# Gate matrices from 64 packed columns: one matmul per token in place of two

## The chip, the cores and the metric

The kernel runs on one core of one Trainium2 chip. The metric is the device time of one execution in microseconds, lower is better. A core has five engines with a queue of their own each: PE (TensorE, matmuls; its weight loads are listed as PEld), DVE (VectorE), ACT (ScalarE), POOL (GpSimd) and SP (SyncE, which issues most of the DMAs here). PE reads SBUF and writes PSUM, which has eight banks of 128 x 512 float32 words.

## The reference

Two layers of a decoder trunk over 1040 positions (16 meta tokens and 1024 real ones) of width 1024. Each layer adds a token mixer (sliding-window attention, stick-breaking attention and gated linear attention side by side) and then a PEER feed-forward block with 4096 experts. Only the second block matters here:

```python
s = einsum('thpd,hpnd->thpn', (xt @ wq).reshape(t, 8, 2, 128), sub_keys)
s_top, i_top = top_k(s, 16)                      # per head, on 64 keys twice
best_s, best_j = top_k(all sums of two of them, 16)
idx = expert numbers of the best 16, for 8 heads   # 128 per token
g = softmax(best_s)
a = gelu((xt @ u.T)[idx]) * g
w = zeros(t, 4096).at[token, idx].add(a)
out = w @ v
```

So each token has 128 chosen experts with a gate each. The kernel computes gelu(xt @ u.T) for all 4096 experts, and multiplies it by a dense gate matrix that is zero but at the chosen experts.

## The kernel before, in words

Matrices are held transposed, with features on the 128 partitions and positions along the free dimension. Float32 products go through three matmuls of rounded high and low parts. The positions of a layer are taken as two halves, each of two quarters: the first half is the object `P` (528 positions in layer 0, 512 in layer 1), the second half `Q` (512). `peer_setup` sets `first` to True for P and to False for Q.

`hidden` (L1117 is its matmul) computes the 4096 expert activations as 32 rows of 128 experts. A row is 24 matmuls of 128 x 512 into one PSUM bank, and then a gelu on ACT into `G`, an array of [128, 32 rows, positions]. For positions whose gates are there already, the gelu goes to a buffer (L1123) and POOL multiplies it by the gates that stand in `G` (L1124); for the others it goes into `G` (L1126). The weights are copied to a rounded form on ACT (L310) as they come in.

`gates` makes the dense gates of 16 positions in one call. An expert number is split in two: m, one of 128 (the partition), and r, one of 32 (the row). The 128 slots of a position (8 heads by 16 choices) lie on the partitions, and for each position a matmul sums over the slots: (slots x 128, a one-hot matrix `Lh` of m) transposed, times (slots x 32, the one-hot matrix `R0` of r times the gate). The gate is held as two float16 numbers, a high and a low part, scaled by 2^15 (`GSC`), so `R` has two parts. DVE builds Lh (L1156, 128 x 2048 float16), R0 (L1159, 128 x 512) and R (L1161, 128 x 1024). PE then does 32 matmuls of 32 columns (L1168), for each position the high and the low part into the same 32 columns of a bank, so that PSUM adds them. One bank holds the 16 positions. DVE multiplies the rows that `hidden` has finished by the gates, straight from PSUM, with the scale taken out (L1173); ACT copies the gates of the later rows into `G` (L1175). Lh, R0 and R have two buffers each; the PSUM ring "g" has banks 0 and 1.

`hidden(l, Q, G, HQ, 32, "hq", cst, QE)` (L1358) calls `gates` after its rows, so many that the 32 calls of the second half are spread evenly over rows 8 to 30; the rows use the ring "hq", banks 4 to 7. Before it `combine` makes m, r and the gates on DVE (its lines L1063 and L1098 write float16 elements that don't lie side by side), and `slots` brings them to the slots' layout. After it `values` multiplies `G` by v, for which all gates must be there.

Each buffer has a fixed place in one of two arenas by a table of names. `s` holds the scores of the product keys, 3072 words; in the last layer the rows `hs` are loaded into its place (L1387) after the second half's scores are done with. The order of the instructions on each engine is not that of the program: a planner orders them by a timeline that it works out itself before the launch. An engine then runs its queue strictly in that order, and an instruction that waits holds up those behind it. Buffers that overlap are kept in the order of the program by waits.

Of the kernel before, what the change touches and what calls it, by code (L numbers as in the profile page):

```python
# [12 lines left out]
F32 = mybir.dt.float32  # L13
F32R = mybir.dt.float32r
F16 = mybir.dt.float16
BF16 = mybir.dt.bfloat16
U32 = mybir.dt.uint32
AF = mybir.ActivationFunctionType
ALU = mybir.AluOpType
# [16 lines left out]
GSC = float(2 ** 15)  # L36
# [23 lines left out]
def tile_trunk(ctx, tc, h0, w_pk, wgate, w2, glab, w_out, wqT, keysT, u_pk, v_w, sinks,  # L60
               n_attn, n_ffn, n_mix, n_fin, out):
    nc = tc.nc
    ACT, DVE, POOL, PE, SP = nc.scalar, nc.vector, nc.gpsimd, nc.tensor, nc.sync
# [9 lines left out]
    place = {}  # L73
    NG = 12

    def lay(ar, plan, o, lim=None):
        for t, e, b in plan:
            e = (e + 7) // 8 * 8
            at = place.setdefault(t, [ar, [], 0])[1]
            while len(at) < b and (lim is None or o + e <= lim):  # L80
                at.append(o)
                o += e
        return o
# [8 lines left out]
    for t in ("ah", "al"):  # L92
# [8 lines left out]
    o = lay(1, [("G", G_EL, 1), ("s", 3072, 1)], g0)  # L101

    o = max(lay(1, [("L", 1024, 2), ("R0", 256, 2), ("R", 512, 2)], o),
            lay(1, [(t, e, 1) for t, e in [("X", 1536), ("C", 768), ("W", 192), ("J", 192), ("qi", 192), ("rmx", 12),
                                           ("rsr", 12)] + [(f"rt{i}", 96) for i in range(8)]], o))
# [13 lines left out]
    kb, bb = place["keep"][1], place["beta"][1]  # L119

    place["h5"] = [1, [place["ht"][1][0] + i * 272 for i in range(5)], 0]
    place["xa"] = [1, [place["fac"][1][0] + i * 272 for i in range(4)], 0]
    place["xb"] = [1, [place["L"][1][0] + i * 272 for i in range(7)], 0]
    place["hs"] = [1, [place["s"][1][0]], 0]
# [14 lines left out]
    def sb(shape, dt, tag, bufs=1):  # L139
        pl = place[tag]  # L140
        off = pl[1][pl[2] % len(pl[1])]
        pl[2] += 1
        n = 1
        for x in shape[1:]:
            n *= x
        words = (n * (2 if dt in (F16, BF16) else 4) + 3) // 4
        assert (dt == F32R) == (pl[0] == 0), tag
        a = arenas[pl[0]][0:shape[0], off:off + words]
        if dt not in (F32, F32R):
            a = a.bitcast(dt)  # L150
        a = a[:, 0:n]
        if len(shape) == 3:
            a = a.rearrange("p (a b) -> p a b", b=shape[2])
        elif len(shape) == 4:
            a = a.rearrange("p (a b c) -> p a b c", b=shape[2], c=shape[3])
        elif len(shape) == 5:
            a = a.rearrange("p (a b c d) -> p a b c d", b=shape[2], c=shape[3], d=shape[4])
        return a
# [4 lines left out]
    def set_rings(**kw):  # L163
        for tag, bs in kw.items():
            rings[tag] = [bs, 0]

    def ps1(tag="a"):
        r = rings[tag]
        r[1] += 1
        return banks[r[0][(r[1] - 1) % len(r[0])]]  # L170

    set_rings(d=(0, 1), o=(2,), a=(3, 4, 5, 6, 7), h=(6, 7, 2, 3), hq=(4, 5, 6, 7), g=(0, 1), s=(4, 5), v=(4, 5, 6, 7, 2, 3))


    ident = const.tile([128, 128], F32, name="ident")
# [762 lines left out]
    def peer_setup(qa, qb, first):  # L938

        P = Layer()  # L940
        P.sp = Span(qa.c0, qb.c1)
        P.parts = [(0, qa), (qa.w, qb)]
        P.merge = qa.w == qb.w
        P.sall = sb([128, 3072], F32, "s")
        P.s0 = sb([128, 1536], F32, "s0")
        P.first = first
        P.mT, P.rT = [[sb([128, 272], F16, t) for i in range(2)] for t in ("mT", "rT")]
        P.gg = [sb([128, 68, 2, 4], F16, "gg") for i in range(2)]
        P.mS = sb([128, 3, 128], F16, "mS")
        P.rS = sb([128, 3, 128], F16, "rS")  # L950
        P.gS = sb([128, 3, 128], F32, "gS")
        P.V = {}
        P.rows = 0
        P.gated = [0, 0]
        return P
# [150 lines left out]
    def hidden(l, P, G, lo, hi, ring, cst=None, end=32):  # L1106

        cs = cuts(P, (0, 1))
        for r in range(lo, hi):
            pss = [ps1(ring)[:, 0:w] for h, o, w in cs]  # L1110
            for k in range(KT):
                if k % 4 == 0:
                    wh, wl = wpiece(u_pk[l, r][:, k * 128:(k + 4) * 128], f"u{l}_{r}_{k // 4}")
                ks = slice(k % 4 * 128, k % 4 * 128 + 128)
                for i, (wt, low) in enumerate(((wh, 0), (wh, 1), (wl, 0))):
                    for ps, (h, o, w) in zip(pss, cs):
                        PE.matmul(ps, wt[:, ks], yv(h, low, k, 0, w // 2 if h is None else w),  # L1117
                                  start=(k == 0 and i == 0), stop=(k == KT - 1 and i == 2))
            for ps, (h, o, w) in zip(pss, cs):
                n = min(max(sum(P.gated) - o, 0), w)  # L1120
                if n:
                    ga = sb([128, w], F32, "h5" if w <= 272 else "ht")
                    ACT.activation(ga[:, 0:n], ps[:, 0:n], AF.Gelu)  # L1123
                    POOL.tensor_tensor(G[:, r, o:o + n], ga[:, 0:n], G[:, r, o:o + n], op=ALU.mult)  # L1124
                if n < w:
                    ACT.activation(G[:, r, o + n:o + w], ps[:, n:w], AF.Gelu)  # L1126
            P.rows = r + 1
            while cst and sum(P.gated) < P.sp.w and sum(P.gated) * (end - lo) < P.sp.w * (r + 1 - lo):
                gates(P, int(P.gated[0] == P.parts[0][1].w), G, *cst)
# [16 lines left out]
    def gates(P, half, G, iotaM, iotaR):  # L1146


        t0 = P.gated[half]
        go = P.parts[half][0] + t0  # L1150

        def v4(a, n):
            return a[:, t0:t0 + 16].rearrange("p (b t) -> p b t", t=4).unsqueeze(2).to_broadcast([128, 4, n, 4])

        Lh = sb([128, 4, 128, 4], F16, "L", 2)
        DVE.tensor_tensor(Lh, iotaM.unsqueeze(1).to_broadcast([128, 4, 128, 4]), v4(P.mT[half], 128), op=ALU.is_equal)  # L1156

        R0 = sb([128, 4, 32, 4], F16, "R0")
        DVE.tensor_tensor(R0, iotaR.unsqueeze(1).to_broadcast([128, 4, 32, 4]), v4(P.rT[half], 32), op=ALU.is_equal)  # L1159
        R = sb([128, 4, 2, 32, 4], F16, "R")  # L1160
        DVE.tensor_tensor(R, R0.unsqueeze(2).to_broadcast([128, 4, 2, 32, 4]),  # L1161
                          P.gg[half][:, t0 // 4:t0 // 4 + 4].unsqueeze(3).to_broadcast([128, 4, 2, 32, 4]), op=ALU.mult)
        n = P.rows
        ps = ps1("g")
        for i in range(16):
            b, t = i // 4, i % 4
            for part in range(2):
                PE.matmul(ps[:, i * 32:(i + 1) * 32], Lh[:, b, :, t], R[:, b, part, :, t], start=(part == 0),  # L1168
                          stop=(part == 1))
        pv = ps.rearrange("p (t r) -> p r t", r=32)  # L1170
        if n:
            gv = G[:, 0:n, go:go + 16]
            DVE.scalar_tensor_tensor(gv, pv[:, 0:n], 1.0 / GSC, gv, op0=ALU.mult, op1=ALU.mult)  # L1173
        if n < 32:
            ACT.activation(G[:, n:32, go:go + 16], pv[:, n:32], AF.Copy, scale=1.0 / GSC)  # L1175
        P.gated[half] = t0 + 16
# [71 lines left out]
    hq = sb([128, KT, 272], F32, "hq")  # L1248
# [22 lines left out]
    for l in range(DEPTH):  # L1271
# [3 lines left out]
        P = peer_setup(qs[0], qs[1], True)  # L1275
# [39 lines left out]
        G = sb([128, 32, 528], F32, "G")  # L1315
# [68 lines left out]
        o, sp = Q.parts[1]  # L1384
# [63 lines left out]
```

## Time and profile before

| | |
|---|---|
| median of 3 runs | 3275.61 us (3270.31 to 3278.28) |
| profiled execution | 3277.03 us, its span 3275.3 us, mean granted clock 0.967 |
| PE busy | 3116.9 us (95%) |
| DVE busy | 2062.4 us (63%) |
| ACT busy | 1368.4 us (42%) |
| POOL busy | 980.8 us (30%) |
| gate matmuls (L1168) | 4128, of which 1024 in the second half of each layer |

Busy times come from one profiled execution. The span runs from the first to the last instruction. An instruction's own time can reach over the start of the next one on the same engine, so busy times of a stretch are less than the sum of the durations. "Idle before" is the time in which the engine did nothing ahead of an instruction, with what ended it.

### The profile page before, as it was taken

The page shows a single profiled execution, that of the slowest core. Times are in us where ns is not written, and L with a number is a line of the kernel's source. Part 1 is how long each engine was busy: PE and PEld are TensorE (multiplying, and loading weights), DVE is VectorE, ACT ScalarE, POOL GpSimd, SP SyncE. Part 2 cuts the span into 40 slices and gives each one's busy share as a digit, 9 for nine tenths or more (in the row PEclk, how much of TensorE's full clock was granted, in tenths as well). Part 3 has the DMA queues.
Part 4 walks back from the last instruction along what each step waited for, and adds up shares of the span by engine and source line. Part 5 has one row for each costly group of instructions (what it writes and reads, how often), then busy time and mean ns, then how long its engine had stood idle before and what let it go on. Part 6 is the DMA issues. An engine that isn't in the chain of part 4 may idle for free.

```text
span 3275.3 us, 65889 instructions
## 1 busy us (share of the span) xinstructions
PE 3116.9 (95%) x23453; PEld 2625.9 (80%) x23453; DVE 2062.4 (63%) x6694; ACT 1368.4 (42%) x3120; POOL 980.8 (30%) x976
## 2 busy tenths in 40 slices
PE   8999999989899999999998999999889999899998
PEld 7686887769899998888885878786768888688788
DVE  4645445689886299763325554558796736986457
ACT  4554434423334344324445544334333344443354
POOL 5314021323455242020501141213144524302136
PEclk9898999989999999999998999999799999999999
DMA  8676775637445665546766887667454467554655
GB/s 269 224 254 213 233 272 177 218 114 252 132 137 185 184 194 185 162 140 204 266 202 194 291 268 243 230 208 229 165 176 142 156 196 229 185 175 142 213 180 168
DMA packets 406443, 655.57 MB, mean 200 GB/s; under 512 B 44560, under 2 KB 122464, under 8 KB 406112
## 3 DMA queue, kind: packets, MB, share of 16 engines
q1 hardware_dynamic: 406112, 651.35, 61.7%
q8 instruction: 184, 3.01, 0.4%
q14 instruction: 147, 1.20, 0.1%
HBM read 492.70 MB, written 158.47 MB: 199 GB/s over the span
## 4 chain that ended last, share of the span: by engine, by line
PE 37%; DVE 9%; DMA 2%; ACT 1%; issue 1%; POOL 0%; SPq 0%; POOLq 0%; DVEq 0%; ACTq 0%
PE b L1207 10%; PE b L1117 9%; PE b L339 7%; PE b L1168 2%; PE b L991 2%; PE b L707 1%; PE b L761 1%; DVE arena_r L1201 1%; DVE arena L1001 1%; PE b L622 1%; DVE arena L1004 1%; DVE arena L1002 1%; DMA arena<-in_v_w_dram 1%; PE b L743 0%; PE b L584 0%
## 5 line engine op out<-in xcount | busy, mean ns | idle before, releaser
L283 POOL TENSOR_TENSOR arena_r<-arena,arena_r 128x512 fp32r<-128x512 f32 (+1 forms) x440 | 568.7, 1297 | 844.7 <-ACT arena_r L276 763.8
L1207 PE MATMUL b<-arena_r 128*128 128x512 f32 (+2 forms) x4224 | 742.1, 335 | 23.7 <-DVE arena_r L1201 17.9
L1117 PE MATMUL b<-arena_r 128*128 128x512 f32 (+2 forms) x3840 | 759.3, 356 | 5.1 <-DVE arena L263 5.1
L1207 PEld LDWEIGHTS b<-arena_r 128*128 128x128 f32 x4224 | 640.0, 189 | 114.1 <-DVE arena_r L1201 25.3
L339 PE MATMUL b<-arena_r 128*128 128x256 f32 (+1 forms) x4992 | 694.9, 294 | 22.7 <-DVE arena L361 6.8
L1117 PEld LDWEIGHTS b<-arena_r 128*128 128x128 f32 x3840 | 623.4, 190 | 102.1 <-DVE arena L263 5.7
L339 PEld LDWEIGHTS b<-arena_r 128*128 128x128 f32 x4992 | 638.2, 194 | 58.9 <-issue 22.9
L276 ACT ACTIVATE arena_r<-arena 128x512 fp32r<-128x512 f32 x456 | 286.1, 629 | 492.5 <-POOL arena_r L283 116.4
L1201 DVE TENSOR_TENSOR arena_r<-arena,arena_r 128x512 fp32r<-128x512 f32 (+2 forms) x352 | 274.1, 794 | 328.8 <-ACT arena_r L1200 328.3
L310 ACT ACTIVATE arena_r<-arena 128x512 fp32r<-128x512 f32 x392 | 246.1, 630 | 432.5 <-issue 132.5
L991 PE MATMUL b<-arena_r 128*128 128x256 f32 (+1 forms) x1632 | 209.1, 283 | 2.7 <-DMA arena_r<-m_0l 1.3
L991 PEld LDWEIGHTS b<-arena_r 128*128 128x128 f32 (+1 forms) x1632 | 197.0, 183 | 12.3 <-issue 4.3
L1124 POOL TENSOR_TENSOR arena<-arena 128x32 f32<-128x32 f32 (+25 forms) x91 | 106.1, 1174 | 286.5 <-ACT arena L1175 261.7
L1156 DVE TENSOR_TENSOR arena<-arena 128x2048 f16<-128x2048 f16 x129 | 171.4, 1331 | 21.4 <-PE b L1168 21.4
L259 POOL TENSOR_TENSOR arena<-arena 128x256 f32<-128x256 f32 (+1 forms) x126 | 110.2, 875 | 248.9 <-ACT arena L258 248.8
L1200 ACT ACTIVATE arena_r<-arena 128x512 fp32r<-128x512 f32 (+2 forms) x352 | 172.1, 502 | 29.8 <-PE b L1207 26.2
L1173 DVE SCALAR_TENSOR_TENSOR arena<-b,arena 128x224 f32<-128x224 f32 (+20 forms) x129 | 63.7, 500 | 151.1 <-PE b L1168 146.8
L1168 PEld LDWEIGHTS <-arena 128*128 128x128 f16 x4128 | 144.2, 118 | 16.9 <-issue 13.7
L719 DVE TENSOR_TENSOR_SCAN arena<-arena,zf 128x272 f32<-128x272 f32 (+6 forms) x116 | 105.1, 908 | 75.1 <-ACT arena L714 74.3
L1168 PE MATMUL b<-arena 128*128 128x32 f16 x4128 | 152.1, 190 | 0.0
L283 DVE TENSOR_TENSOR arena_r<-arena,arena_r 128x256 fp32r<-128x256 f32 (+1 forms) x140 | 75.3, 541 | 98.5 <-ACT arena_r L276 87.3
L580 POOL TENSOR_TENSOR arena<-arena,mhalf 128x8 f32<-128x8 f32 (+3 forms) x43 | 62.7, 1459 | 231.3 <-DVE arena L577 150.9
(269 smaller groups left out, 3826.3 us busy)
## 6 DMA issues: line engine op xcount, KB each, us to landing
arena<-in_v_w_dram SPq DMA_DIRECT2D x288, 256.0 KB, 2.9
arena<-in_u_pk_dram SPq DMA_DIRECT2D x256, 256.0 KB, 3.0
arena<-in_w_pk_dram SPq DMA_DIRECT2D x144, 256.0 KB, 4.6
arena_r<-a_0l SPq DMA_DIRECT2D x108, 256.0 KB, 4.0
arena_r<-a_1l SPq DMA_DIRECT2D x108, 256.0 KB, 3.8
arena<-m SPq DMA_DIRECT2D x96, 256.0 KB, 4.4
arena<-h SPq DMA_DIRECT2D x192, 128.0 KB, 3.2
arena_r<-a_0h SPq DMA_DIRECT2D x72, 256.0 KB, 3.5
```

Source lines behind the costliest of these rows:

```text
L259: POOL.tensor_tensor(acc, acc, sq[:, 0:sp.w], op=ALU.add)
L276: ACT.activation(hi, src, AF.Copy)
L283: e.tensor_tensor(lo[:, a:b], src[:, a:b], hi[:, a:b].bitcast(F32), op=ALU.subtract)
L310: ACT.activation(hi, wload(src), AF.Copy)
L339: PE.matmul(ps, wt[:, ks], x.at(low, k, xo, sp.w), start=(k == 0 and i == 0), stop=(k == KT - 1 and i == 2))
L991: PE.matmul(ps, yv(half, low, k, o, m), wt[:, kk * 256:kk * 256 + 256], start=(k == 0 and i == 0 and e == 0), stop=(k == KT - 1 and i == 2 ...
L1117: PE.matmul(ps, wt[:, ks], yv(h, low, k, 0, w // 2 if h is None else w), start=(k == 0 and i == 0), stop=(k == KT - 1 and i == 2))
L1156: DVE.tensor_tensor(Lh, iotaM.unsqueeze(1).to_broadcast([128, 4, 128, 4]), v4(P.mT[half], 128), op=ALU.is_equal)
L1168: PE.matmul(ps[:, i * 32:(i + 1) * 32], Lh[:, b, :, t], R[:, b, part, :, t], start=(part == 0), stop=(part == 1))
L1200: ACT.activation(ah, G[:, r, o:o + w], AF.Copy)
L1201: last = DVE.tensor_tensor(al, G[:, r, o:o + w], ah.bitcast(F32), op=ALU.subtract)
L1207: PE.matmul(ps, wt[:, d * 128:d * 128 + 128], pr[low], start=(opens and r == 0 and i == 0), stop=(closes and r == 31 and i == 2))
```

## The change

For the second halves (`P.first` is False) only:

- R is laid out as [128, 4 blocks, 4 positions, 64], the 32 columns of the high part and the 32 of the low part of a position side by side. The multiply that writes it has the same inputs and the same order of elements (block, part, r, position), so it now writes with a step of 64 elements in its innermost dimension.
- One matmul for each position with 64 columns in place of two with 32; the two parts come out side by side, not added up.
- The 16 positions fill two banks, eight in each, from a ring "gq" of banks 0 to 3.
- ACT copies the high part of each bank into a new buffer S (`gsum`, two buffers of 512 words at the start of `s`), scaled; DVE adds the low part, scaled, from PSUM.
- The multiply of the finished rows and the copy of the later rows read S in place of PSUM.

```diff
+    place["gsum"] = [1, [place["s"][1][0], place["s"][1][0] + 512], 0]
...
-    set_rings(d=(0, 1), o=(2,), a=(3, 4, 5, 6, 7), h=(6, 7, 2, 3), hq=(4, 5, 6, 7), g=(0, 1), s=(4, 5), v=(4, 5, 6, 7, 2, 3))
+    set_rings(d=(0, 1), o=(2,), a=(3, 4, 5, 6, 7), h=(6, 7, 2, 3), hq=(4, 5, 6, 7), g=(0, 1), gq=(0, 1, 2, 3), s=(4, 5), v=(4, 5, 6, 7, 2, 3))
...
-        R = sb([128, 4, 2, 32, 4], F16, "R")
-        DVE.tensor_tensor(R, R0.unsqueeze(2).to_broadcast([128, 4, 2, 32, 4]),
+        if P.first:
+            R = sb([128, 4, 2, 32, 4], F16, "R")
+            Rw = R
+        else:
+            R = sb([128, 4, 4, 64], F16, "R")
+            Rw = R.rearrange("p b t (a r) -> p b a r t", a=2)
+        DVE.tensor_tensor(Rw, R0.unsqueeze(2).to_broadcast([128, 4, 2, 32, 4]),
                           P.gg[half][:, t0 // 4:t0 // 4 + 4].unsqueeze(3).to_broadcast([128, 4, 2, 32, 4]), op=ALU.mult)
         n = P.rows
+        if not P.first:
+            S = sb([128, 16, 32], F32, "gsum")
+            for e in range(2):
+                ps = ps1("gq")
+                for i in range(8):
+                    b, t = (8 * e + i) // 4, i % 4
+                    PE.matmul(ps[:, i * 64:(i + 1) * 64], Lh[:, b, :, t], R[:, b, t, :], start=True, stop=True)
+                pv = ps.rearrange("p (t a r) -> p t a r", a=2, r=32)
+                Se = S[:, 8 * e:8 * e + 8]
+                ACT.activation(Se, pv[:, :, 0], AF.Copy, scale=1.0 / GSC)
+                DVE.scalar_tensor_tensor(Se, pv[:, :, 1], 1.0 / GSC, Se, op0=ALU.mult, op1=ALU.add)
+            pv = S.rearrange("p t r -> p r t")
+            gv = G[:, 0:n, go:go + 16]
+            DVE.tensor_tensor(gv, pv[:, 0:n], gv, op=ALU.mult)
+            if n < 32:
+                ACT.activation(G[:, n:32, go:go + 16], pv[:, n:32], AF.Copy)
+            P.gated[half] = t0 + 16
+            return
```

## Rows read from the trace of the kernel before

**Rows 1.** The page: busy time by engine; shares of the chain that ended last

```profile
PE 3116.9 (95%) x23453; PEld 2625.9 (80%) x23453; DVE 2062.4 (63%) x6694; ACT 1368.4 (42%) x3120; POOL 980.8 (30%) x976
...
PE 37%; DVE 9%; DMA 2%; ACT 1%; issue 1%; POOL 0%; SPq 0%; POOLq 0%; DVEq 0%; ACTq 0%
```

**Rows 2.** L1168 in 1300 to 1800 us: duration ns min/median/max, first and last start

```profile
L1168 PE MATMUL b<-arena x1024: 188/190/209, 1343.5 to 1479.2; 128*128 128x32 f16 x171
```

**Rows 3.** Busy us by stretch: start:end length, PE, PEld, DVE, ACT, POOL; clock, DMA

```profile
1280.00:1343.00 63.00, 63.00 (x278) 50.38 (x276) 60.65 (x311) 30.62 (x53) 3.33 (x7) 1.00 0.62 194
1343.00:1480.00 137.00, 137.00 (x1461) 113.89 (x1460) 84.29 (x124) 42.98 (x105) 26.23 (x25) 1.00 0.45 142
...
2927.00:3064.00 137.00, 137.00 (x1462) 113.89 (x1461) 84.28 (x123) 43.51 (x106) 24.71 (x22) 1.00 0.44 141
```

**Rows 4.** The chain that ended last, in order of time: start us, length us

```profile
2937.40 5.88 PE b L1117 x25
...
3063.97 5.67 PE b L1117 x24
```

**Rows 5.** Timeline of one period: start us, length us, engine, line [idle before <-releaser]

```profile
1399.48 2.21 PEld L1168 LDWEIGHTS <-arena 128*128 128x128 f16 x64 [0.27 <-issue]
...
1400.84 0.44 DVE L1173 SCALAR_TENSOR_TENSOR arena<-b,arena 128x272 f32<-128x272 f32 x1 [2.73 <-PE b L1168]
1401.20 1.22 DVE L1156 TENSOR_TENSOR arena<-arena 128x2048 f16<-128x2048 f16 x1
...
1401.64 6.27 PE L1117 MATMUL b<-arena_r 128*128 128x512 f32 x26
...
1402.33 1.13 DVE L1161 TENSOR_TENSOR arena<-arena 128x1024 f16<-128x1024 f16 x1
...
1404.99 0.68 DVE L1161 TENSOR_TENSOR arena<-arena 128x1024 f16<-128x1024 f16 x1
1405.60 0.75 DVE L1159 TENSOR_TENSOR arena<-arena 128x512 f16<-128x512 f16 x2
...
1407.75 2.22 PEld L1168 LDWEIGHTS <-arena 128*128 128x128 f16 x64 [0.27 <-issue]
```

**Rows 6.** L1161 over the whole span: duration ns min/median/max, first and last start

```profile
L1161 DVE TENSOR_TENSOR arena<-arena x129: 675/689/1789, 858.7 to 3054.2; 128x1024 f16<-128x1024 f16 x129
```

**Rows 7.** Groups by shape in 1343 to 1481 us: busy us, mean ns | idle before

```profile
L1156 DVE TENSOR_TENSOR arena<-arena 128x2048 f16<-128x2048 f16 x30 | 37.5, 1250 | 0.0
...
L1161 DVE TENSOR_TENSOR arena<-arena 128x1024 f16<-128x1024 f16 x30 | 27.3, 909 | 0.0
...
L1173 DVE SCALAR_TENSOR_TENSOR arena<-b,arena 128x256 f32<-128x256 f32 x2 | 0.8, 418 | 2.9 <-PE b L1168 2.9
...
L1173 DVE SCALAR_TENSOR_TENSOR arena<-b,arena 128x496 f32<-128x496 f32 x1 | 0.7, 673 | 4.9 <-PE b L1168 4.9
```

**Rows 8.** DVE's groups by shape over the span, copies with scattered 16-bit writes

```profile
L1063 DVE CAST arena<-arena 128x128 f16<-128x128 uint32 x14 | 6.3, 450 | 0.0
L1098 DVE COPY arena<-arena 128x128 f16<-128x128 f16 x14 | 6.1, 439 | 0.1
...
L1063 DVE CAST arena<-arena 128x192 f16<-128x192 uint32 x2 | 1.2, 606 | 0.0
...
L1098 DVE COPY arena<-arena 128x192 f16<-128x192 f16 x2 | 1.1, 570 | 0.0
```

**Rows 9.** ACT's groups by shape over the span, PSUM to SBUF

```profile
L1126 ACT ACTIVATE arena<-b 128x256 f32<-128x256 f32 x26 | 9.9, 382 | 0.0
```

**Rows 10.** The loads of hs: issue ns min/median/max, first and last start

```profile
L1387 SPq DMA_DIRECT2D arena<-h x8: 319/320/860, 2739.7 to 2845.9; - x8
```

**Rows 11.** A thin stretch of attention: columns as in rows 3

```profile
2293.00:2313.00 20.00, 19.34 (x77) 10.95 (x79) 11.29 (x21) 6.34 (x13) 2.07 (x5) 0.50 0.02 7
```

## The prediction

> **What bounds the kernel now.** I read the page first: PE is busy 95% of the span, DVE 63%, and the chain that ended last runs through PE far more than through any other engine [rows 1]. So a microsecond taken from PE is worth a microsecond, as long as PE stays the engine that is waited for. The change sits in one stage that comes once in each layer, and there the averages over the span say little. I therefore asked for the stage by itself. The 1024 gate matmuls of layer 0's second half start at 1343.5 us and end at 1479.2 [rows 2], which is 32 calls of `gates` at 32 matmuls; layer 1's lie at 2927 to 3064, as many. The busy times of these two stretches [rows 3] are the base of the sum: PE 137.0 of 137 us, DVE 84.3 (62%), ACT 43, POOL 25 to 26, clock 1.00. In the stretch just before (1280 to 1343) DVE is at 60.65 of 63, so no DVE work can be moved ahead out of the stage. The chain of waits goes through this stage on PE alone, by the matmuls of `hidden` [rows 4].
>
> A row-by-row look at one period [rows 5] shows how the engines fit. PE loads 64 gate weights in 2.21 us (two calls), then does some 26 `hidden` matmuls in 6.27 us, and the next pair of calls comes 8.27 us after the first (1399.48 to 1407.75). In this period DVE evacuates two calls (L1173), builds Lh twice (L1156), R twice (L1161) and R0 twice (L1159), and then waits 2.73 us for PE. DVE has some 3 us to spare in each period; that is all the cover there is for new DVE work.
>
> **The change part by part.** Durations are of the profiled execution, 3277.03 us with its span of 3275.3; that is 1.4 us above the median of the runs, which I neglect.
>
> PE: 32 matmuls of 32 columns become 16 of 64. A pair of load and matmul takes 2.21/64 = 34.6 ns now [rows 5], so a call takes 1.11 us. No row shows 64 columns of 16-bit data. If the wider matmul costs nothing more, a call takes 16 x 34.6 = 0.55 us; if each column costs what it costs between 32 and 512 columns, (6270/26 - 34.6)/480 = 0.43 ns, it takes 16 x (34.6 + 13.8) = 0.77. The gain is 0.34 to 0.56 us a call, 11 to 18 us in each stage, so PE would need 119 to 126 us. I take the smaller gain.
>
> DVE, the multiply that writes R (L1161): its inputs and its 1024 elements stay, but the four neighbours that it writes one after the other now lie 64 elements (128 bytes) apart. Today it takes 0.689 us at the median [rows 6] and 0.909 us in the mean of this stage [rows 7]. The 0.22 us between them go with POOL's transfers of the gelu rows: the L1161 at 1402.33 took 1.13 us, the one at 1404.99 0.68 [rows 5]. For 16-bit writes that aren't neighbours, the trace has copies in `combine`: 439 ns for 128 elements and 570 for 192 on L1098, 450 and 606 on L1063 [rows 8], which is 2.05 and 2.44 ns for each further element. For 1024 elements they give 439 + 896 x 2.05 = 2.28 us and 450 + 896 x 2.44 = 2.64. From below: the evacuation L1173, of whose operands none is 16-bit, goes from 418 ns at 256 elements to 673 at 496 [rows 7], 1.06 ns an element, so 418 + 768 x 1.06 = 1.23 us; and 0.69 if nothing changes. I take 2.28, because L1098 is nearest in kind: 16-bit in, 16-bit out, neighbours in time 32 bytes apart in place. With the 0.22 us for POOL, and 0.09 us less because the next instruction starts that much before the last one has ended (0.69 long, next one 0.60 later, [rows 5]), a build costs 2.41 us in place of 0.82, that is 1.59 more.
>
> The Trainium skill, page "VectorE: DVE Perf Modes", section "What auto-detection actually checks", says that two elements a cycle are had only where every tensor is 16-bit with a step of one; the new write isn't. By the formula of the same page for one element a cycle, (N + 151)/0.96 (section "The TRN2 errata — SBUF-src ops pay a fixed extra latency per instruction"), the multiply would take 1.22 us, an estimate, and the sum below would be that of rival A. The rule speaks against the change, as rows 8 do, but at half their price.
>
> DVE, the evacuation: two additions of 128x256 from PSUM are new. L1173 has that size at 418 ns [rows 7]; less the overlap, 0.75 us for both. The final multiply keeps its n x 16 elements and reads S in place of PSUM; I cost it as before (from -0.1 to +0.2 us a call, since both inputs now come from SBUF and can meet POOL).
>
> ACT: two copies of 128x256, 382 ns each [rows 9], 24 us a stage on an engine that is busy 43 of 137; hidden by its idle time. The final copy moves from PSUM to S at the same size. But each addition waits for its copy, and the copy for the first or last eight matmuls; behind a waiting addition DVE's queue holds the next builds. Where DVE is behind, the matmuls and copies of a call are done before DVE comes to its additions, so I price this wait at nothing within the stage, and at some 2 us at its end, where the last call's matmuls, two copies, two additions and multiply come one after the other, and `values` needs all gates.
>
> PSUM: four banks in place of two let the two halves of two calls be in flight; 2 and 3 are idle in this stage. S: `gsum` lies in the first 1024 words of `s`, where `hs` is loaded later. These eight loads go out at 2739 to 2846 us now [rows 10], long before the last gates of layer 1; four of them must now wait until after 3064. They are first needed at the end of the first pass of `values`, tens of microseconds later, so 0; if one stands in SP's queue ahead of the weights of `values`, these wait with it, 1 to 3 us once.
>
> **The sum.** A stage holds 30 builds (L1156 x30; two are made ahead) and 32 evacuations. DVE: 84.3 + 30 x 1.59 + 32 x 0.75 = 84.3 + 47.7 + 24.0 = 156.0 us. PE: 126. So DVE takes PE's place as the engine that is waited for, PE stands at each pair of calls until R is written, and its gain is not seen at all. With 2 us at the end the stage takes 158 in place of 137, 21 more; two stages 42. The two builds made ahead (2 x 1.59 us, on a DVE that is 96% busy) may add up to 3 us a layer; I leave them to the range. 3277 + 42 = 3319 us. With the smaller ends (R at 2.28 and no POOL, 0.65 for the additions) DVE needs 84.3 + 41 + 21 = 146, and the total is 3277 + 2 x 11 = 3299; with 2.64 for R and 0.2 us more a call, 84.3 + 59 + 30 = 173, and 3353.
>
> **Rivals.** (A) The write goes at one element a cycle. For it: L1173 [rows 7]. Against it: both copies of [rows 8] show twice that, and which of the two holds decides the sign of the whole change. The page of the Trainium skill named above stands on this rival's side, with no word on scattered writes. R then costs 1.23 + 0.22 - 0.09 = 1.36, a build 0.54 more, and DVE needs 84.3 + 16 + 24 = 124.5, PE 119 to 126. PE stays the bound, at 95% and more on both, with a few microseconds of waits between them: 127 to 134 a stage, 3 to 10 less, and the time is 3257 to 3271, middle 3264. It is faster up to the point where DVE's added work passes some 50 us a stage, 1.6 us a call.
> (B) DVE is the bound, and its queue stands still besides. The planner orders DVE and ACT by a timeline of its own, which may hold the strided multiply for cheap; then an addition stands ahead of builds that could run, its copy behind an ACT weight copy L310 that waits for PE. Price: one ACT copy (0.38 us) to one L310 (0.63) each call, 12 to 20 us a stage; 3343 to 3359. For it: ACT's L310 waits on PE in this stage; against it: DVE late means copies early.
> (C) PE standing 2 us in each period lowers its clock, as in a thin stretch of attention, where the granted clock was 0.50 [rows 11], that is 1.2 GHz. The `hidden` matmuls (137 less 32 x 1.11, 101 us a stage) would take up to twice that; a stage 200 and more, 3400. Against it: PE still works some three quarters of the time here.
> (D) Nothing measurable: the two effects cancel, DVE at 135 to 140.
>
> **How the numbers follow.** My forecast with its own range of 3299 to 3340: 0.56. B 0.13, C 0.03. A 0.20, of which a quarter ends within 0.3%, about what a measurement of this kernel can tell from no change (10 us). D 0.08, of which a quarter is on the slower side and a quarter on the faster. Slower: 0.56 + 0.13 + 0.03 + 0.02 = 0.74; same: 0.05 + 0.04 = 0.09; faster: 0.15 + 0.02 = 0.17. The range leaves out C, the far end of B and the lower part of A: 3260 to 3350.
>
> **What would show it.** Right: L1161's counterpart at 2.2 to 2.7 us with 128x1024 elements in the second-half stages and 0.69 to 1.1 in the first-half ones; DVE above 90% of the stage, its waits for PE gone; PE idle before the gate matmuls, released by DVE's R line; both stages some 158 us long, the rest of the kernel where it was. Wrong: that multiply at 1.2 to 1.4 us, PE busy without a gap, stages of 127 to 134 us. If the stage is long and DVE idle for 15 us and more, B is at work. If PE's 16 matmuls take more than 0.8 us a call, the PE term is mis-sized.

## The result, and the profile after

The changed kernel takes 3476.27 us at the median (3474.29 to 3478.55, 4 runs), the kernel before 3275.79 beside it: a ratio of 1.0614, 95% interval 1.0595 to 1.0633, 200 us more. Slower was forecast, but by 43 us; the range ended at 3350.

The page of the profiled execution (3475.38 us, span 3473.7) shows where to look. Against [rows 1], PE's busy time is 32 us more, DVE's 310 us more, and the chain that ended last has moved from PE to DVE.

```profile
PE 3148.5 (91%) x22429; PEld 2642.8 (76%) x22429; DVE 2372.8 (68%) x6822; ACT 1419.5 (41%) x3249; POOL 1034.0 (30%) x976
...
PE 27%; DVE 17%; DMA 3%; ACT 1%; issue 1%; POOL 1%; SPq 0%; POOLq 0%; DVEq 0%; ACTq 0%
```

The gate matmuls of the second halves, now L1177, run from 1339.2 to 1573.0 us and from 3027.5 to 3260.5. The stages that took 136 us take 234 and 233; these 195 us are nearly all of the span's 198. Busy times of the two stretches, with columns as in [rows 3]:

```profile
1339.00:1574.00 235.00, 155.50 (x970) 123.96 (x968) 231.27 (x191) 69.18 (x170) 52.22 (x24) 0.81 0.29 88
...
3027.00:3261.00 234.00, 155.02 (x974) 123.64 (x973) 229.78 (x191) 70.06 (x171) 59.62 (x21) 0.82 0.29 89
```

PE and DVE have changed places: DVE is busy 231 of 235 us, PE 155. The clock, 1.00 in [rows 3], is 0.81. The groups of the first of the two stages name the line (busy us, mean ns of one | idle before):

```profile
L1167 DVE TENSOR_TENSOR arena<-arena 128x1024 f16<-128x1024 f16 x31 | 149.1, 4808 | 0.0
L1118 PE MATMUL b<-arena_r 128*128 128x512 f32 x454 | 131.2, 453 | 1.1 <-ACT arena L1127 1.1
...
L1181 DVE SCALAR_TENSOR_TENSOR arena<-b,arena 128x256 f32<-128x256 f32 x62 | 30.6, 525 | 1.3 <-ACT arena L1180 1.3
L1177 PE MATMUL b<-arena 128*128 128x64 f16 x512 | 28.8, 217 | 77.3 <-DVE arena L1181 67.2 <-DVE arena L1167 10.0
...
L1184 DVE TENSOR_TENSOR arena<-arena 128x336 f32<-128x336 f32 x2 | 1.5, 758 | 0.0
```

The multiply that writes R takes 4808 ns in place of 909 [rows 7]: same inputs, same 1024 elements, another step of the write. It alone is 149 us of the stage. PE stands 77 us before the gate matmuls (L1177): 67.2 of them for an addition (L1181), which stands behind a build of R in DVE's queue, and 10.0 for the build itself. The timeline shows the new order of things:

```profile
1442.40 8.75 PE L1118 MATMUL b<-arena_r 128*128 128x512 f32 x30
...
1444.86 4.90 DVE L1167 TENSOR_TENSOR arena<-arena 128x1024 f16<-128x1024 f16 x1
...
1449.32 0.70 DVE L1181 SCALAR_TENSOR_TENSOR arena<-b,arena 128x256 f32<-128x256 f32 x1
...
1451.37 4.74 DVE L1167 TENSOR_TENSOR arena<-arena 128x1024 f16<-128x1024 f16 x1
...
1456.42 1.01 PE L1177 MATMUL b<-arena 128*128 128x64 f16 x16 [4.46 <-DVE arena L1181]
...
1457.24 8.19 PE L1118 MATMUL b<-arena_r 128*128 128x512 f32 x30
```

In [rows 5] DVE stood 2.73 us in a period of 8.27 and waited for PE. Now a period is 14.8 us (1442.40 to 1457.24), DVE does not stand, and PE stands 4.46 us before a call. The chain of waits in the other stage, which was L1117 on PE every 8 us [rows 4], is now this multiply, twice in each period:

```profile
3044.27 4.86 DVE arena L1167
...
3050.51 4.65 DVE arena L1167
...
3059.97 4.83 DVE arena L1167
...
3066.18 4.64 DVE arena L1167
```

### The profile page after: what moved, and what is told of

It is laid out like the page before. It is cut to its first block, busy times and chain, and to the rows that moved or that the text cites. A ratio compares the mean times of both kernels' runs of the same rounds, so it can differ in the third digit from the quotient of the medians.

```text
span 3473.7 us, 64065 instructions
## 1 busy us (share of the span) xinstructions
PE 3148.5 (91%) x22429; PEld 2642.8 (76%) x22429; DVE 2372.8 (68%) x6822; ACT 1419.5 (41%) x3249; POOL 1034.0 (30%) x976
## 3 DMA queue, kind: packets, MB, share of 16 engines
q14 instruction: 149, 1.22, 0.1%
## 4 chain that ended last, share of the span: by engine, by line
PE 27%; DVE 17%; DMA 3%; ACT 1%; issue 1%; POOL 1%; SPq 0%; POOLq 0%; DVEq 0%; ACTq 0%
PE b L1232 9%; PE b L340 6%; DVE arena L1167 4%; PE b L1118 4%; PE b L992 1%; DVE arena L1157 1%; PE b L1193 1%; PE b L708 1%; PE b L762 1%; DVE arena L1002 1%; DVE arena L1005 1%; DVE arena L1003 1%; DVE arena_r L1226 1%; PE b L623 1%; DMA arena<-in_v_w_dram 1%
## 5 line engine op out<-in xcount | busy, mean ns | idle before, releaser
L284 POOL TENSOR_TENSOR arena_r<-arena,arena_r 128x512 fp32r<-128x512 f32 (+1 forms) x440 | 559.7, 1276 | 853.0 <-ACT arena_r L277 773.3
L1118 PE MATMUL b<-arena_r 128*128 128x512 f32 (+2 forms) x3840 | 799.1, 369 | 6.3 <-DVE arena L264 5.2
L1232 PE MATMUL b<-arena_r 128*128 128x512 f32 (+2 forms) x4224 | 747.1, 336 | 23.2 <-DVE arena_r L1226 16.2
L1118 PEld LDWEIGHTS b<-arena_r 128*128 128x128 f32 x3840 | 656.2, 199 | 114.3 <-DVE arena L264 5.9
L1232 PEld LDWEIGHTS b<-arena_r 128*128 128x128 f32 x4224 | 642.6, 189 | 116.5 <-DVE arena_r L1226 25.1
L340 PEld LDWEIGHTS b<-arena_r 128*128 128x128 f32 x4992 | 638.0, 194 | 60.9 <-issue 20.7
L1167 DVE TENSOR_TENSOR arena<-arena 128x1024 f16<-128x1024 f16 x129 | 381.2, 2955 | 0.1
L1125 POOL TENSOR_TENSOR arena<-arena 128x32 f32<-128x32 f32 (+25 forms) x91 | 170.2, 1880 | 429.5 <-ACT arena L1186 428.4
L1177 PE MATMUL b<-arena 128*128 128x64 f16 x1024 | 58.4, 218 | 155.7 <-DVE arena L1181 137.4
L1177 PEld LDWEIGHTS <-arena 128*128 128x128 f16 x1024 | 50.5, 123 | 169.6 <-issue 150.0
```

Of the source, the lines that this page charges most:

```text
L284: e.tensor_tensor(lo[:, a:b], src[:, a:b], hi[:, a:b].bitcast(F32), op=ALU.subtract)
L340: PE.matmul(ps, wt[:, ks], x.at(low, k, xo, sp.w), start=(k == 0 and i == 0), stop=(k == KT - 1 and i == 2))
L1167: DVE.tensor_tensor(Rw, R0.unsqueeze(2).to_broadcast([128, 4, 2, 32, 4]), P.gg[half][:, t0 // 4:t0 // 4 + 4].unsqueeze(3).to_broadcast([12 ...
L1232: PE.matmul(ps, wt[:, d * 128:d * 128 + 128], pr[low], start=(opens and r == 0 and i == 0), stop=(closes and r == 31 and i == 2))
```

## The experiments

The theory: the scattered write of R makes DVE the bound of the stage, and all 200 us come from DVE's extra work there. Open was why the write costs 4.5 ns an element where the copies of [rows 8] gave 2.05; whether the evacuation or the lower clock have a part; and whether PE's gain is there to be had at all.

**The write's step, by itself.** The kernel before, with multiplies in front that differ only in where they write. The third argument of `rp` is the step of the write in elements; `rr` writes in R's own pattern with that many elements from one position to the next. `oh` is 16-bit, `of` float32.

```diff
+    for rep in range(3):
+        DVE.tensor_tensor(oh[:, 0:1024], i0, i1, op=MU)
+        DVE.tensor_tensor(rp(oh, 512, 2, 2), r2(i0, 2), r2(i1, 2), op=MU)
...
+        DVE.tensor_tensor(rp(oh, 16, 64, 64), r2(i0, 64), r2(i1, 64), op=MU)
...
+        DVE.tensor_tensor(rp(oh, 16, 68, 64), r2(i0, 64), r2(i1, 64), op=MU)
...
+        DVE.tensor_tensor(rr(64), r5(i0), r5(i1), op=MU)
...
+        DVE.tensor_tensor(rr(68), r5(i0), r5(i1), op=MU)
...
+        DVE.tensor_tensor(of[:, 0:1024], f0, f0, op=MU)
+        DVE.tensor_tensor(rp(of, 32, 32, 32), r2(f0, 32), r2(f0, 32), op=MU)
...
```

> The kernel before, with DVE multiplies of 1024 elements put ahead of everything else, three times each, that differ only in the step of the write (16-bit or float32); nothing else is changed. Theory 1 (the step decides: a step of 128 bytes is the worst case): 16-bit writes with small steps near 2 ns an element (2.2 us), with 128 bytes 4.5 ns (4.7 us), with 136 and 144 bytes back near 2.2 us; R's own pattern 4.7 us at a pitch of 64 and 2.2 at 68. Theory 2 (any scattered 16-bit write in a multiply of two inputs costs this): 4.7 us at every step of 4 bytes and more. Theory 3 (the runs of four neighbours are the cause): only R's own five-dimensional pattern costs 4.7 us, at every pitch, and the others 2.2.

The instructions by line, duration in ns min/median/max. In order: neighbours, steps of 2, 4, 8, 64 and 68 elements, R's pattern at 64 and at 68, then float32 with neighbours and with a step of 128 bytes:

```profile
L1266 DVE TENSOR_TENSOR arena<-arena x3: 691/691/2044, 6.3 to 235.9; 128x1024 f16<-128x1024 f16 x3
L1267 DVE TENSOR_TENSOR arena<-arena x3: 1292/1296/1319, 8.4 to 236.7; 128x1024 f16<-128x1024 f16 x3
L1268 DVE TENSOR_TENSOR arena<-arena x3: 2420/2429/2429, 12.7 to 238.0; 128x1024 f16<-128x1024 f16 x3
L1269 DVE TENSOR_TENSOR arena<-arena x3: 4683/4685/4690, 15.6 to 240.4; 128x1024 f16<-128x1024 f16 x3
...
L1272 DVE TENSOR_TENSOR arena<-arena x3: 4712/4716/4718, 29.9 to 254.3; 128x1024 f16<-128x1024 f16 x3
...
L1274 DVE TENSOR_TENSOR arena<-arena x3: 4640/4640/4641, 41.1 to 263.7; 128x1024 f16<-128x1024 f16 x3
...
L1282 DVE TENSOR_TENSOR arena<-arena x3: 4710/4715/5274, 87.3 to 301.4; 128x1024 f16<-128x1024 f16 x3
...
L1284 DVE TENSOR_TENSOR arena<-arena x3: 4695/4695/5212, 98.5 to 310.9; 128x1024 f16<-128x1024 f16 x3
...
L1287 DVE TENSOR_TENSOR arena<-arena x3: 1202/1226/1227, 113.6 to 324.8; 128x1024 f32<-128x1024 f32 x3
L1288 DVE TENSOR_TENSOR arena<-arena x3: 1900/1900/1966, 115.4 to 326.0; 128x1024 f32<-128x1024 f32 x3
```

Theory 1 falls: 128 bytes is no special step. Of the write steps not shown (from 16 to 160 elements) the fastest takes 4435 and the slowest 5270 ns at the median. So from 8 elements (16 bytes) on every step costs 4.4 to 5.3 us; at 2 and 4 elements it costs 1.3 and 2.4. Theory 3 falls as well: R's pattern costs no more than the plain one. Theory 2 comes nearest, though not from 4 bytes on: from 16.

**R's positions 136 bytes apart, in the changed kernel.**

```diff
-    o = max(lay(1, [("L", 1024, 2), ("R0", 256, 2), ("R", 512, 2)], o),
+    o = max(lay(1, [("L", 1024, 2), ("R0", 256, 2), ("R", 544, 2)], o),
...
-            R = sb([128, 4, 4, 64], F16, "R")
+            R = sb([128, 4, 4, 68], F16, "R")[:, :, :, 0:64]
```

> The changed kernel with R's positions 68 elements apart in place of 64 (136 bytes in place of 128). Theory 1 (128 bytes is the worst case): the multiply falls from 4.82 to some 2.3 us, a stage from 234 to some 158 us, and the time from 3476 to 3300 to 3330. Theories 2 and 3: the multiply stays at 4.8 us and the time at 3476 within 10.

3472.20 us, 1.061 of the kernel before (1.059 to 1.063); the multiply at 4812 ns (median of layer 0). The step of 128 bytes is ruled out in the kernel too.

**R's new layout alone.** The matmuls are again 32 of 32 columns that add up in a bank, and the evacuation is that of before.

```diff
-        if not P.first:
+        if False:
...
-                PE.matmul(ps[:, i * 32:(i + 1) * 32], Lh[:, b, :, t], R[:, b, part, :, t], start=(part == 0),
+                PE.matmul(ps[:, i * 32:(i + 1) * 32], Lh[:, b, :, t], (R[:, b, part, :, t] if P.first else R[:, b, t, part * 32:part * 32 + 32]), start=(part == 0),
```

> The changed kernel with R's new layout alone: matmuls of 32 columns that add up in one bank, and the evacuation, are those of before. If the write of R is the cause, DVE needs 30 x (1.14 + 0.34 + 4.75) + 32 x 0.45, 201 us a stage, and the time is 3277 + 2 x 66, 3395 to 3420. If the larger part lies in the evacuation (additions, reads of S) or in PE's lower clock, under 3360.

3425.90 us, 1.046 (1.044 to 1.048), 6 us above the expected range. The write alone brings 150 of the 200 us. DVE is busy 210 of the 212 us of this stage:

```profile
1336.00:1548.00 212.00, 166.79 (x1469) 135.82 (x1469) 210.48 (x140) 45.05 (x112) 70.16 (x22) 0.88 0.33 101
```

PE, at 167 us, waits there for the build itself. The other 50 us come with the rest of the change, that is with the evacuation, since DVE is the bound and it gives DVE the only other new work: 50/64 calls, 0.78 us each.

**R as before, the rest of the change kept.** PE reads the 64 columns with a step of four elements.

```diff
...
-            R = sb([128, 4, 4, 64], F16, "R")
-            Rw = R.rearrange("p b t (a r) -> p b a r t", a=2)
...
+        R = sb([128, 4, 2, 32, 4], F16, "R")
...
-                    PE.matmul(ps[:, i * 64:(i + 1) * 64], Lh[:, b, :, t], R[:, b, t, :], start=True, stop=True)
+                    PE.matmul(ps[:, i * 64:(i + 1) * 64], Lh[:, b, :, t], R[:, b].rearrange("p a r t -> p (a r) t")[:, :, t], start=True, stop=True)
```

> The changed kernel with R written as before (16-bit neighbours side by side); the 64 columns of a matmul are read with a step of four elements over both parts. All else of the change stays. If the write of R is the whole loss, DVE needs 84 + 24 = 108 us a stage, PE 119 to 126 is the bound again, and the time is 3241 to 3255. If the additions and the reads of S hold up the queues by themselves, no gain is left: 3270 to 3290.

3273.72 us, 0.9992 (0.9977 to 1.0007): the whole loss is gone, so nothing of it came from the evacuation while PE was the bound. But no gain is left either. The time lies in the second of the two ranges, but that is luck, for its reason is not the right one: DVE is at 111 of 137 us, as expected, and PE does not stand at all; it is PE's own work that has not become less. Busy times of the stage, and two calls on PE (start us, length us):

```profile
1343.00:1480.00 137.00, 137.00 (x946) 113.21 (x945) 111.25 (x181) 72.95 (x170) 23.84 (x28) 1.00 0.46 147
```

```profile
1402.90 2.15 PE L1172 MATMUL b<-arena 128*128 128x64 f16 x32
```

Two calls take 2.15 us with 32 matmuls, where 64 took 2.31 in the kernel before (at 1399.48; its loads 2.21, [rows 5]). So a matmul of 64 columns costs 67 ns, nearly twice the 36 of one of 32, when its columns lie 8 bytes apart.

**Which writes cost this.** Again instructions in front of the kernel before. Those below write 16-bit elements 32 bytes apart, except one (the last multiply), which reads with a step of 8 bytes and writes neighbours.

```diff
...
+        DVE.tensor_copy(rp(oh, 1024, 16), r2(i0, 1024, 16))
...
+        DVE.tensor_tensor(rp(oh, 128, 16), r2(i0, 128, 16), r2(i1, 128, 16), op=MU)
...
+        DVE.tensor_tensor(rp(oh, 1024, 16), r2(i0, 1024, 16), r2(i1, 1024, 16), op=MU)
...
+        DVE.tensor_scalar(rp(oh, 1024, 16), r2(i0, 1024, 16), 2.0, None, op0=MU)
...
+        DVE.tensor_copy(rp(oh, 1024, 16), r2(f0, 1024, 16))
+        DVE.tensor_tensor(r2(oh, 1024, 4), rp(i0, 1024, 4), r2(i1, 1024, 4), op=MU)
...
```

> The kernel before, with instructions put ahead of everything else, three times each, that write 16-bit elements 32 bytes apart; nothing else is changed. It asks why copies of 128 and 192 elements gave 2.05 ns for each further element and the multiply of 1024 takes 4.5. Theory 1 (the number of elements: the first writes of an instruction are taken up by a buffer): a copy of 1024 takes some 4.5 us too, and eight copies of 128 back to back start some 0.55 us apart. Theory 2 (the operation: a multiply of two inputs pays twice): the copy of 1024 takes 2.3 us, and a multiply of 128 some 0.7 us in place of 0.44. Theory 3 (16-bit sources): copies and multiplies with float32 sources go at 2.2 us for 1024, those with 16-bit sources at 4.5.

In order: copy of 1024, multiply of 128, multiply of 1024, multiply by a constant, copy from float32, multiply that reads with a step (ns min/median/max):

```profile
L1264 DVE COPY arena<-arena x3: 2309/2336/2575, 11.5 to 121.9; 128x1024 f16<-128x1024 f16 x3
...
L1266 DVE TENSOR_TENSOR arena<-arena x3: 686/695/1231, 15.9 to 124.7; 128x128 f16<-128x128 f16 x3
...
L1269 DVE TENSOR_TENSOR arena<-arena x3: 4426/4439/4439, 20.4 to 129.0; 128x1024 f16<-128x1024 f16 x3
...
L1271 DVE TENSOR_SCALAR arena<-arena x3: 2308/2320/2453, 25.6 to 134.2; 128x1024 f16<-128x1024 f16 x3
...
L1274 DVE CAST arena<-arena x3: 2304/2312/2322, 39.3 to 145.5; 128x1024 f16<-128x1024 f32 x3
L1275 DVE TENSOR_TENSOR arena<-arena x3: 1202/1226/1228, 43.4 to 147.9; 128x1024 f16<-128x1024 f16 x3
```

Theory 2 holds to the number, and what counts is the number of sources, for the multiply by a constant costs no more than the copy. With one source a scattered 16-bit element costs 2.1 ns at any count (the copy of 1024 is what [rows 8] extrapolate to), with two sources (4439 - 695)/896 = 4.2 ns. The source's type doesn't matter. Why a second source doubles the price of a write was not traced. A stepped read of one source costs less than a stepped write: at 8 bytes 1.23 us where the write took 2.43, at 128 bytes 1.89 where it took 4.72 (all but the 1.23 from the run on the write's step).

**The same in the changed kernel.** The multiply writes neighbours, and a copy of one source scatters them.

```diff
...
-            Rw = R.rearrange("p b t (a r) -> p b a r t", a=2)
+            Rw = sb([128, 4, 2, 32, 4], F16, "Rt")
...
+            DVE.tensor_copy(R.rearrange("p b t (a r) -> p b a r t", a=2), Rw)
```

> The changed kernel with R made in two steps: the multiply writes neighbours as before, and a copy then brings the 1024 elements to the packed places, 128 bytes apart. One instruction more on DVE, the same scattered write. If a scattered 16-bit write costs two cycles an element from one source and four from two: 0.69 to 0.91 + 2.31 us in place of 4.81, DVE 48 to 54 us a stage less, the time 3365 to 3385. If the scattered write costs the same whoever does it, the copy comes on top: 3510 to 3530.

3375.09 us, 1.031 (1.028 to 1.035). One more instruction on the engine that is the bound, and 101 us less than the change. The copy and the multiply (the latter with the first halves' builds among them):

```profile
L1172 DVE COPY arena<-arena x64: 2474/2623/2735, 1327.6 to 3149.6; 128x1024 f16<-128x1024 f16 x64
...
L1168 DVE TENSOR_TENSOR arena<-arena x129: 668/693/1792, 848.7 to 3145.2; 128x1024 f16<-128x1024 f16 x129
```

**R written in runs of 32, read with a step.**

```diff
-            Rw = R.rearrange("p b t (a r) -> p b a r t", a=2)
+            Rw = R.rearrange("p b t (a r) -> p b a t r", a=2)
...
+            r0 = r0.rearrange("p b r t -> p b t r")
+            for a in range(2):
+                DVE.tensor_tensor(Rw[:, :, a], r0, g0[:, :, a].unsqueeze(3).to_broadcast([128, 4, 4, 32]), op=ALU.mult)
```

> The changed kernel with R written in runs of 32 neighbours, by two multiplies of 512 elements that read R0 with a step of 8 bytes; R's layout, PE and the evacuation stay those of the change. If the scattered write is the whole loss: two multiplies at 0.6 to 0.75 us, DVE 84 + 30 x 0.5 + 32 x 0.9 = 128 us a stage, PE 119; DVE and PE are about level, 3250 to 3275. If scattered reads cost as much as scattered writes: 3400 and more.

3278.05 us, 1.0012 (0.9996 to 1.0027), just above the expected range and no difference that is measured. The two multiplies take 713 ns each. PE has its gain (32 matmuls take 1.24 us at 1413.25), but DVE has become as long as PE, and each waits for the other: both are busy some 126 of the 137 us, and PE stands some 8 us before the gate matmuls for additions.

```profile
1343.00:1480.00 137.00, 126.89 (x975) 102.56 (x973) 125.77 (x217) 70.86 (x171) 23.72 (x24) 0.98 0.49 154
```

```profile
L1174 DVE TENSOR_TENSOR arena<-arena 128x512 f16<-128x512 f16 x62 | 41.7, 713 | 0.0
```

**R written in order, by operands of step one.** The gates and the r numbers are held twice each, side by side, so that the innermost pair of every operand lies together.

```diff
...
+            R0 = sb([128, 16, 16, 2], F16, "R0")
+            DVE.tensor_tensor(R0, iota1.unsqueeze(1).to_broadcast([128, 16, 16, 2]),
+                              P.rT2[half][:, t0:t0 + 16].unsqueeze(2).to_broadcast([128, 16, 16, 2]), op=ALU.is_equal)
+            R = sb([128, 16, 64], F16, "R")
+            for a in range(2):
+                DVE.tensor_tensor(R[:, :, 32 * a:32 * a + 32].rearrange("p t (c e) -> p t c e", e=2), R0,
+                                  P.gg2[half][:, t0:t0 + 16, a].unsqueeze(2).to_broadcast([128, 16, 16, 2]), op=ALU.mult)
...
```

> A version that keeps 64 side-by-side columns and writes them in order: the gates and the r numbers of the second half are held twice each, side by side, so that R0 and R are built with steps of one in all operands; the evacuation stays that of the change. R0 at 0.41 and R as two multiplies of 0.41 us. DVE needs 84 + 5 + 32 x 0.9 = 118 us a stage, PE 137 - 32 x 0.55 = 119. If PE's gain is had, 3245 to 3260; if the two level engines hold each other up, 3265 to 3280.

3251.53 us, 0.9923 (0.9907 to 0.9939): faster than both kernels, as expected. Its stage (1341.4 to 1465.2) has PE at 124 and DVE at 112 of 125 us, the multiplies of R at 433 ns each, and two calls of 16 matmuls take 1.25 us:

```profile
1341.00:1466.00 125.00, 124.42 (x969) 100.71 (x967) 112.15 (x215) 70.37 (x171) 23.62 (x24) 1.00 0.51 161
```

```profile
L1186 DVE TENSOR_TENSOR arena<-arena 128x512 f16<-128x512 f16 x61 | 24.0, 433 | 0.0
```

```profile
1410.96 1.25 PE L1196 MATMUL b<-arena 128*128 128x64 f16 x32
```

**The same for both halves.** The edit takes away the conditions on `P.first`; the first half's calls use the ring "g" with its two banks. The first half's S, and a part of its doubled gates, now lie in `s` as well.

> The ordered write and the packed 64 columns for the gates of both halves (the first half with two banks). In the first-half stretches of the kernel before, DVE is at 133 of 161 us and 106 of 136, and POOL at 92 and 69. If PE is still the bound there, another 0.55 us for each of 65 calls: 3215 to 3235. If DVE, with 0.9 us a call more (133 + 31 = 164 of 161 less 18) and POOL beside it, becomes the bound in layer 0 and level in layer 1: 3250 to 3275.

3333.93 us, 1.016 (1.013 to 1.020), slower than either of my two numbers: the first-half gate stretches grow, in layer 0 from 161 to 164 us (877.6 to 1041.8) and in layer 1 from 136 to 190 (2484.8 to 2674.7), and the stretches from there to the second halves' gates grow by 17 and 14 us. In the first DVE is nearly full, at 158 of 174 us. In the second neither engine is full:

```profile
876.00:1050.00 174.00, 146.71 (x1444) 143.00 (x1443) 157.55 (x242) 77.34 (x204) 83.53 (x64) 0.88 0.37 120
2490.00:2680.00 190.00, 132.64 (x900) 105.32 (x899) 133.05 (x215) 69.04 (x163) 66.94 (x52) 0.79 0.31 103
```

In the second DVE stands 59 us for gate matmuls and PE 41 us for additions, so the two engines take turns. What holds them up there, the two banks, the planner's order or the places shared with `s`, was not tried.

## Why the prediction was wrong

The mechanism was the one that was forecast, with most of its signs: L1161's counterpart grew in the second halves alone, DVE is above 90% of the stage, PE is idle before the gate matmuls and released by DVE, and the rest of the kernel is where it was. One sign came otherwise: PE waited mostly for the addition behind the build (67 of 77 us), not for R's line. The step that failed is "For 1024 elements they give 439 + 896 x 2.05 = 2.28 us" and the choice of that price ("I take 2.28"): the term was mis-sized, at 4.81 us measured. The rows were read rightly, and a copy of 1024 elements does take 2.3 us. But I took "nearest in kind" by the type of the elements and overlooked that L1098 and L1063 have one source and the multiply has two; with two sources the same write costs twice as much. A build costs 3.9 us more (4.81 less 0.91), not 1.59; 30 of them are 117 us in place of 47.7, and this gap of 69 us is nearly all of the 75 between the 156 us of DVE work in the sum and the 231 measured. The run with R's layout alone bears it out: there DVE's work in the stage, 84 us before, is 210, and with the rest of the change it is 231, 21 us more where the sum had 24.

The other terms, by the same steps:

- The additions, 0.75 us a call: 0.78 from the difference between the change and R's layout alone. This holds the reads of S as well, which I had priced at nothing and which cost something: L1184 takes 758 ns for 128x336, L1173 took 502 from PSUM.
- PE, 0.55 to 0.77 us a call: it lies nearer the lower end. With R in order, 16 matmuls of 64 columns take 0.63 (half of 1.25), and 32 of 32 columns took 1.16 (half of 2.31) by the same reading, 0.53 less. Having taken the smaller gain, I had PE need 126 where 120 would have done; with DVE as the bound it made no difference. In the change itself PE is busy 28.8/32 = 0.90 us a call, above the 0.8 that I had named as a sign; but there the clock is 0.81 and calls stop half-way for an addition, so this is not the price of the matmuls. The Trainium skill, page "TensorE: Matmul & The Clock Gate", section "Back-to-back issue gap", gives one price for all matmuls of 1 to 64 columns. The trace agrees that the two widths cost the same where the 64 columns lie side by side (1.25 us for 32 matmuls of either width), not where they lie 8 bytes apart (2.15).
- The rule of the Trainium skill that I weighed (page "VectorE: DVE Perf Modes", section "What auto-detection actually checks") gives two elements a cycle to 16-bit tensors with a step of one; at one a cycle I had worked out 1.22 us, an estimate. The measured time is near it for a read with a step of 8 bytes (1.23) and for a write with a step of 4 (1.30); for the scattered write it is nearly four times that (4.44 to 4.81), and the measurement decides. So rival A, at 3264, was further off than my forecast.
- Rival B is out: DVE stood 4 us in a stage. Rival C has half come true: the clock fell to 0.81 and the `hidden` matmuls went from 399 to 453 ns, but PE, at 155 of 235 us, was not the bound. The row that I had named for C [rows 11] has PE busy 19.34 of 20 us, so it shows a low clock, but not that standing brings it; in the change's stage PE stood 77 us before gate matmuls, at 0.81. The run with the copy fits a bound on DVE: 4.81 - 0.69 - 2.62 = 1.50 us less for R in each call took 101 us away, 1.58 for each of 64 calls, as a sum over DVE alone would have it.
- Loads of `hs` did move behind the last gates (the last one from 2845.9 to 3265.4 us). Stage lengths leave 198 - 195 = 3 us for them, the builds made ahead and all else.

Where PE's gain went has three answers. In the change it stands in the shadow of DVE. With R written as before it doesn't arise, because then PE pays for the stepped read. With R written in runs of 32 it arises, but DVE, at 126 us, is then as long as PE. Of these runs only the one with R written in order, where DVE needs 112 us, shows a gain in the time: two stages with (2.31 - 1.25)/2 x 32 = 17 us less of gate matmuls each brought 24 us of 34. By the pages PE is busy 29.9 us less (3116.9 to 3087.0) and stands 5.6 us more. One place where it stands is the end of the stage: before, a row of 24 `hidden` matmuls (1479.26, 5.83 us) still came behind the last gate matmuls of layer 0; now all rows come ahead of them, and after the last gate matmuls (1464.69) PE stands 1.72 us for an addition. In the stretch that follows, to 1600, the clock is 0.96, where it was 1.00. The rest of the 10 us was not traced.

## What to carry to other kernels

A layout that spares one engine has to be written by another: price the write with a row of the same number of sources, the same type and the same step, and if there is none, let the range reach well beyond the price of the nearest row (here twice it was needed). Before the bound engine is relieved, compare the slack of the next one (here 53 us a stage) with every instruction that the relief puts on it. When a packed operand is wanted, make the operands that build it fit the order in which it lies, even at the cost of holding them twice.

## What the runs showed of the hardware that was not expected

- DVE, 16-bit elements written one by one: 1.3 us for 1024 at a step of 4 bytes, 2.4 at 8, 4.7 at 16, 4.4 to 5.3 from there to 320 bytes (two sources). One source: 2.3 at 32 bytes. Float32 at 128 bytes, two sources: 1.9 in place of 1.23. ACT (one source) took 4.48 and POOL (two) 4.47 us for the 1024 elements at 32 bytes; no run has the same with neighbours on these two.
- PE, reading 64 16-bit columns 8 bytes apart, took 1.7 times as long as with 64 side by side (2.15 against 1.25 us for 32 matmuls); for 32 columns the step of the read made no difference (1.25 us for 32 matmuls at 8 bytes, 1.24 side by side).
- POOL is slower beside a scattered write of DVE: L1125 took 4.02 us for 128x256 in the change's stage, 1.10 in the run with R in runs of 32, and L1124 1.27 for the same shape before.
